# Norms behind the out-projection, a buffer for the meta keys, and three steps of linear attention on ScalarE

## The chip, the core and the metric

The kernel runs on one core of a Trainium2 chip. Its engines are TensorE (PE, with its weight loads as PEld), VectorE (DVE), ScalarE (ACT), GpSimd (POOL) and SyncE (SP, which issues nearly all DMAs). The metric is the device time of one execution in microseconds. Every matmul of a projection works in float32 precision by splitting each operand into a rounded high part and a low rest and adding three products.

## The reference

Sixteen meta tokens are put ahead of 2048 tokens of width 1024, and two layers follow, each with a residual and a layer norm:

```
conv layer:  u = h @ w_in + b_in;  a, ga, z = split(u, 3)
             c = causal depthwise conv, 31 taps, of a * sigmoid(ga)
             y = (silu(layer_norm(c)) * silu(z)) @ w_out + b_out
GLA layer:   q, k, v, r, a1 = split(h @ w_in);   4 heads, 128 wide in q and k, 256 in v
             g = log_sigmoid(a1 @ w_a2 + b_a) / 16;   b = cumsum of g in a chunk of 64
             o = (q exp(b)) @ S + att @ v,  att[t,s] = sum_d q k exp(b_t - b_s), s <= t
             S = exp(b_last) S + (k exp(b_last - b)).T @ v     (chunk by chunk)
             o = o * rsqrt(mean(o*o) + 1e-6) * norm_g;  y = (o * silu(r)) @ w_out
both:        h = layer_norm(alpha * h + y);   the meta tokens are dropped at the end
```

## The kernel before

The program has four phases. In phase 1 (to about 555 us) the input projection and the convolution run, and their results `c` and `silu(z)` go to DRAM (`c_d`, `sz_d`), channels on partitions. Phase 2 (about 555 to 783 us) takes 17 tiles of tokens (`SUBS`: 16 of 128 and one of 16). Phase 3 (to about 1544 us) is the GLA layer without its out-projection, and phase 4 does that and the last norm.

A tile of phase 2 goes through these steps. `norm` loads `c`, sums over the 8 channel groups (DVE for even tiles, POOL's `tree` for odd ones) and over partitions by a matmul with a constant matrix (`mean`), subtracts, squares on ACT, sums again (POOL), gets the variance by a matmul (L330), forms the reciprocal root on POOL, puts it on a diagonal `dg`, and spreads it over partitions by the matmul `rb` (L335); DVE multiplies `c` by it (L336). `gate` does eight Silus on ACT (L351), multiplies with `silu(z)` on DVE (L354) and splits the product into `h_gt` (ACT, L73) and `l_gt` (DVE, L74). `out_proj` multiplies both by the weights (tiles `pj_y`, 48 matmuls of 512 columns for a tile of tokens, L106 to L108), adds the residual (L377) and does the post-LN (L385 to L398), whose result is stored to `h1_d`. The loop L428 to L435 writes these steps down in the order norm of a later tile, gate of a later tile, out-projection of this one; `head` has by then written down three norms (CB is 4) and one gate.

Phase 3 has 4 blocks of tokens (528, then 3 of 512) and 4 heads, so 16 units, named block_head. `proj_units` writes down the projections and, interleaved, a generator `gla_units` is stepped; two numbers (GRATE, VCOST) set how often. A unit computes the decays (`gl` and `b`: L634 to L638), for block 0 the state after the 16 meta tokens (`khm`, through a transpose into `dsm`), then `kh` (decayed keys, filled on POOL at L683, multiplied on DVE at L685, transposed by PE as `pk`, split into `k_h` and `k_l`), the state products `ds`, the attention matrix in levels (`A`, POOL, ACT and DVE at L719 to L723; `att` and `red`), their sum `at` (L770, L771), its split `a_h`, `a_l`, and the outputs `o` in two halves of two chunks. Each chunk's squares are summed on ACT (L783) into a scratch that is the front of `kh`. `osb` is normalised (L784 to L789) and transposed by PE (`oT`, L794).

In what order an engine runs its instructions is set by a scheduler at compile time, which goes by the order in which they are written down, by the tile pools' buffers (a tag with `bufs=1` has one buffer) and by its own model of costs. On the chip each engine keeps that order and waits on semaphores.

Of the kernel before, what the change touches and what calls it, by code (L numbers as in the profile page):

```python
# [11 lines left out]
F32 = mybir.dt.float32  # L12
F32R = mybir.dt.float32r
AF = mybir.ActivationFunctionType
ALU = mybir.AluOpType
# [34 lines left out]
class Trunk:  # L50
# [349 lines left out]
    def phase2(self, x_tok, wo, rows, h1_d, tail):  # L400
        nc = self.nc
        left = ExitStack()
        wop = self.pool(left, name="p2w", bufs=1)
        const = self.pool(left, name="p2c", bufs=1)
        tp = self.pool(left, name="p2t", bufs=3)
        sm = self.pool(left, name="p2n", bufs=4)
        self.pm.append(self.pool(self.st2, name="p2q", bufs=1, space=PSUM, side="right"))

        w = self.load_out_w(wo, wop, lambda k: self.raw(f"wo{k}")[:, :D] if k < 2 else self.wrp.tile([P, D], F32, tag="wr", name=f"wor{k}"), "wo")
        self.st2w.close()  # L410
        rb = []
        for i in range(3):
            t = const.tile([P, D], F32, name=f"row{i}")
            nc.sync.dma_start(t, rows[i : i + 1].broadcast_to([P, D]))
            rb.append(t)
        b_out, g1, b1 = rb

        def out_proj(i, h, l):
            t0, m = SUBS[i]
            xt = tp.tile([P, D], F32, tag="xt", name=f"xt{i}")  # L420
            nc.sync.dma_start(xt[:m], x_tok[t0 : t0 + m])
            self.out_tile(h, l, w, xt, m, f"y{i}")
            nc.gpsimd.tensor_tensor(xt[:m], xt[:m], b_out[:m], op=ALU.add)
            self.post_ln(sm, xt, m, g1, b1, f"a{i}")
            nc.sync.dma_start(h1_d[t0 : t0 + m], xt[:m])

        ns = len(SUBS)
        for i in range(ns):  # L428
            self.norm_next()
            self.gate_next()  # L430
            if self.nnorm == ns and not self.normed and self.st2:
                self.st2.close()
                self.st2 = None
                tail()
            out_proj(*self.gated.popleft())  # L435
        left.close()


# [18 lines left out]
    def phase3_init(self, wa2, pp, og_d):  # L457
        nc = self.nc
        self.og_d = og_d
        c0 = self.pool(self.st3, name="p3a", bufs=1)  # L460
        self.a1x = [c0.tile([P, P], F32, name=f"a1x{i}") for i in range(2)]
        for t in self.a1x:
            nc.gpsimd.memset(t, 0.0)
        self.hp = self.pool(self.st3, name="p3h", bufs=2)
        c = self.pool(self.st3, name="p3c", bufs=1)
        self.prm = c.tile([P, 8], F32, name="prm3")
        nc.sync.dma_start(self.prm[:, 0:6], pp)
        nc.vector.tensor_scalar(self.prm[:, 6:8], self.prm[:, 4:6], 0.5, None, op0=ALU.mult)

        raw = self.raw("a2")[:, :512]  # L470
        nc.sync.dma_start(raw, wa2)
        self.wa2 = c.tile([P, 512], F32R, name="a2")
        nc.scalar.activation(self.wa2, raw, AF.Copy)
        nc.vector.tensor_tensor(self.wa2[64:96], raw[64:96], self.wa2[64:96], op=ALU.subtract)
        with ExitStack() as st:
            self.gla_consts(c, self.pool(st, name="p3k", bufs=1))
        self.gp = self.pool(self.st3, name="p3g", bufs=2)
        self.S = {}
# [147 lines left out]
    def gates(self, bi, h, hd, ns):  # L626
        nc, n = self.nc, BLOCKS[bi][1]
        gl = self.hp.tile([P, BMAX], F32, tag="gl", name=f"gl{bi}_{h}", bufs=1)
        b = hd["b"] = self.hp.tile([P, BMAX], F32, tag="b", name=f"b{bi}_{h}")
        ba = self.prm[:, h : h + 1]  # L630
        for c0, m in ns:
            ps = self.pjt(f"z{bi}_{h}_{c0}")[:, :m]
            nc.tensor.matmul(ps, lhsT=self.wa2[:, h * P : (h + 1) * P], rhs=self.ah[:, c0 : c0 + m], start=True, stop=True)
            nc.vector.tensor_scalar(gl[:, c0 : c0 + m], ps, ba, 0.0, op0=ALU.add, op1=ALU.min)  # L634
            nc.scalar.activation(b[:, c0 : c0 + m], ps, AF.Abs, bias=ba)
        nc.scalar.activation(b[:, :n], b[:, :n], AF.Exp, scale=-1.0)
        nc.scalar.activation(b[:, :n], b[:, :n], AF.Ln, bias=1.0)
        nc.vector.tensor_tensor(gl[:, :n], gl[:, :n], b[:, :n], op=ALU.subtract)  # L638
        o = n - 512
        rs = self.reset.rearrange("p a b -> p (a b)")  # L640
        if o:
            nc.vector.tensor_tensor_scan(b[:, :o], rs[:, :o], gl[:, :o], 0.0, op0=ALU.mult, op1=ALU.add)
        nc.vector.tensor_tensor_scan(b[:, o : o + 512], rs, gl[:, o : o + 512], 0.0, op0=ALU.mult, op1=ALU.add)
# [7 lines left out]
    def gla_units(self, h, hd, bi, t0, n):  # L651
# [3 lines left out]
        off = n - 512  # L655
        if off:

            kh = self.gp.tile([P, 512], F32, tag="kh", name=f"khm{h}", bufs=1)[:, :off]
            nc.gpsimd.tensor_tensor(kh, b[:, off - 1 : off].to_broadcast([P, off]), b[:, :off], op=ALU.subtract)
            ex(kh, kh)  # L660
            nc.vector.tensor_tensor(kh, kh, k_[:, :off], op=ALU.mult)
            pt = self.pt.tile([P, 4, P], F32, tag="g", name=f"ptm{h}")
            nc.tensor.transpose(pt[:off, 0], kh, K.ident)
            kt = self.gp.tile([NMETA, P], F32, tag="ktm", name=f"ktm{h}", bufs=1)
            nc.scalar.activation(kt, pt[:off, 0], AF.Copy)
            ds = self.pa.tile([P, 4, P], F32, tag="ds", name=f"dsm{h}").rearrange("p a b -> p (a b)")[:, :256]
            nc.tensor.matmul(ds, lhsT=kt, rhs=hd["vm"], start=True, stop=True)
            S = self.S[h] = self.gp.tile([P, 256], F32, tag=f"S{h}", name=f"Sm{h}", bufs=1)
            nc.vector.tensor_copy(S, ds)
            yield  # L670
# [79 lines left out]
        for c2 in range(2):  # L750
            sm = self.pt.tile([P, 2, 144], F32, tag="g", name=f"sm{nm}_{c2}")

            for c in range(2):
                a = (2 * c2 + c) * P
                blocks = [(s, slice(a + s, a + s + 32)) for s in range(0, P, 32)]
                for i, m in enumerate((8, 4, 2)):
                    for s, w in blocks:
                        nc.tensor.matmul(sm[s : s + 32, c, 48 + 32 * i : 80 + 32 * i], lhsT=lv[m][:, w], rhs=lv[m][:, w], start=True, stop=True, skip_group_check=True)
                for s, w in blocks:
                    nc.tensor.matmul(sm[s : s + 32, c, :48], lhsT=ks[:, w], rhs=A1[:, (a + s) // 32], start=True, stop=True, skip_group_check=True)  # L760
            ms = self.gp.tile([P, 2, 144], F32, tag="ms", name=f"ms{nm}_{c2}")
            nc.vector.tensor_tensor(ms, sm, K.lmask.unsqueeze(1).to_broadcast([P, 2, 144]), op=ALU.mult)
            rd = red[:, 2 * c2 : 2 * c2 + 2]
            nc.vector.tensor_reduce(rd, ms[:, :, 16:].rearrange("p c (l t) -> p c t l", t=32), axis=mybir.AxisListType.X, op=ALU.add)
            odd = rd.rearrange("p c (s u) -> p c s u", u=2)[:, :, :, 1]
            nc.vector.tensor_tensor(odd, odd, ms[:, :, :16], op=ALU.add)
            yield
        at = self.gp.tile([P, 4, 4, 32], F32, tag="at", name=f"at{nm}", bufs=1)
        for c in range(4):
            nc.vector.tensor_tensor(at[:, c], red[:, c].unsqueeze(1).to_broadcast([P, 4, 32]), K.blk, op=ALU.mult)  # L770
        nc.vector.tensor_tensor(at, at, att.rearrange("p c (a b) -> p c a b", b=32), op=ALU.add)  # L771
        ath, atl = self.pair3("a", at.rearrange("p c a b -> p c (a b)"), nc.gpsimd, nm, 1)
        yield
        yield
# [1 line left out]
        sq = self.gp.tile([P, 3, 4], F32, tag="sq", name=f"sq{nm}")  # L776
        junk = kh[:, :256]
        for c2 in range(2):
            o2 = self.pt.tile([P, 2, 256], F32, tag="g", name=f"o{nm}_{c2}")
            for c in (2 * c2, 2 * c2 + 1):  # L780
                o = o2[:, c % 2]
                self.mm3(o, [(qh[:, c], ql[:, c], *Ss[c]), (ath[:, c], atl[:, c], vh[:, c], vl[:, c])])
                nc.scalar.activation(junk, o, AF.Square, accum_out=sq[:, 0, c : c + 1])  # L783
            nc.vector.tensor_copy(osb[:, 2 * c2 : 2 * c2 + 2], o2)  # L784
            yield
        nc.vector.tensor_scalar(sq[:, 1], sq[:, 0], 1.0 / 256, RMS_EPS, op0=ALU.mult, op1=ALU.add)
        nc.gpsimd.tensor_tensor(sq[:, 2], sq[:, 1], self.mhalf, op=ALU.pow)
        for c in range(4):
            nc.vector.tensor_scalar(osb[:, c], osb[:, c], sq[:, 2, c : c + 1], None, op0=ALU.mult)  # L789
        yield  # L790
        for e in range(2):
            pt = self.pt.tile([P, 4, P], F32, tag="g", name=f"oT{nm}_{e}")
# [165 lines left out]
```

## Time and profile before

| | |
|---|---|
| median of 3 runs | 1737.01 us (1736.24 to 1739.46) |
| the profiled execution | 1736.39 us, span 1734.4 us |
| mean granted TensorE clock | 0.992 of full speed |
| PE busy | 1679.1 us, 97% |
| DVE, POOL, ACT busy | 1396.5 us, 938.4 us, 841.4 us |

The span runs from the first instruction to the last. Busy times of engines overlap, so they don't add up. The clock is a share of 2.4 GHz; its lower level is 1.2 GHz. In the views below, a wait is idle time of an engine that ended when the named instruction of another one was done. A name such as `pj_y` in the trace stands for all buffers of that name, so a tile's number doesn't show there; it is found by counting.

### The profile page before, as it was taken

To read this page: it belongs to the slowest core of one execution; us is meant where nothing else is said; L and a number is where in the kernel's file an instruction comes from. 1 tells how busy PE (TensorE), PEld (TensorE's weight loads), DVE (VectorE), ACT (ScalarE), POOL (GpSimd) and SP (SyncE) were. 2 spreads that over 40 slices of the span, in tenths; PEclk is the share of its full clock that TensorE was granted. 3 is DMA by queue.
4 is the path that set the end of the run, shared out by engine and by line. 5 is a ranking of instruction groups with operands and counts; after the bars stand their busy time and mean duration, and the time that the engine had idled before them with its cause. 6 is when DMAs were issued, how large, how long until landed. Compare 5 with 4: busy or idle time off the path is not lost.

```text
span 1734.4 us, 29031 instructions
## 1 busy us (share of the span) xinstructions
PE 1679.1 (97%) x11715; PEld 1491.7 (86%) x11715; DVE 1396.5 (81%) x1869; ACT 841.4 (49%) x1269; POOL 938.4 (54%) x675
## 2 busy tenths in 40 slices
PE   8999999999998998999999999999999999999998
PEld 8999999999998776778888888888888888788886
DVE  5789999999998898877776787777887788787665
ACT  6445555655544544445545454555555465541000
POOL 1879999999985788766332243332443153331000
PEclk9999999999999999999999999999999999999999
DMA  7110111111146644443122322223223322355441
GB/s 247 37 37 37 37 69 42 74 52 59 72 146 206 207 148 142 142 139 106 50 86 87 111 84 88 74 87 111 78 75 106 123 74 84 126 170 169 147 134 61
DMA packets 103910, 178.72 MB, mean 103 GB/s; under 512 B 8624, under 2 KB 68400, under 8 KB 103776
## 3 DMA queue, kind: packets, MB, share of 16 engines
q1 hardware_dynamic: 103776, 176.86, 30.4%
q8 instruction: 92, 1.51, 0.4%
q14 instruction: 42, 0.34, 0.1%
HBM read 134.70 MB, written 42.14 MB: 102 GB/s over the span
## 4 chain that ended last, share of the span: by engine, by line
PE 69%; DVE 12%; POOL 8%; ACT 5%; issue 3%; DMA 3%; SPq 0%; DVEq 0%; POOLq 0%; ACTq 0%
PE pj_y L106 4%; PE pj_y L108 4%; PE pj_y L107 4%; PE pj_g L107 3%; PE pj_g L108 3%; PE pj_g L106 3%; PE pj_z L107 3%; PE pj_z L106 3%; PE pj_a L107 3%; PE pj_a L106 3%; PE pj_z L108 3%; PE pj_a L108 3%; POOL A L720 1%; POOL A L719 1%; PE att L729 1%
## 5 line engine op out<-in xcount | busy, mean ns | idle before, releaser
L196 POOL TENSOR_TENSOR gacc<-gacc,prod 128x1024 f32<-128x1024 f32 (+1 forms) x156 | 385.9, 2477 | 63.1 <-ACT prod L195 54.2
L204 DVE SCALAR_TENSOR_TENSOR cacc<-glu,prm,cacc 128x1024 f32<-128x1024 f32 (+1 forms) x292 | 374.8, 1294 | 7.0
L195 ACT ACTIVATE prod<-glu,prm 128x1024 f32<-128x1024 f32 (+1 forms) x156 | 179.1, 1155 | 107.7 <-POOL gacc L196 107.3
L719 POOL TENSOR_TENSOR A<-b 128x256 f32<-128x256 f32 x96 | 80.2, 836 | 269.9 <-PE att L729 105.6
L106 PE MATMUL pj_g<-xh,h_w 128*128 128x412 f32 (+1 forms) x320 | 113.7, 355 | 5.6 <-ACT h_w L73 4.2
L107 PE MATMUL pj_g<-xl,h_w 128*128 128x412 f32 (+1 forms) x320 | 113.5, 355 | 0.3 <-DVE xl L74 0.3
L108 PE MATMUL pj_y<-woh,l_gt 128*128 128x512 f32 (+1 forms) x272 | 109.0, 406 | 4.3 <-DVE l_gt L74 4.2
L106 PE MATMUL pj_y<-woh,h_gt 128*128 128x512 f32 (+1 forms) x272 | 110.7, 410 | 1.9 <-ACT h_gt L73 1.8
L108 PE MATMUL pj_g<-xh,l_w 128*128 128x412 f32 (+1 forms) x320 | 112.5, 353 | 0.0
L107 PE MATMUL pj_z<-xl,h_w 128*128 128x412 f32 (+1 forms) x320 | 112.3, 351 | 0.0
L106 PE MATMUL pj_z<-xh,h_w 128*128 128x412 f32 (+1 forms) x320 | 112.2, 351 | 0.0
L107 PE MATMUL pj_a<-xl,h_w 128*128 128x412 f32 (+1 forms) x320 | 112.2, 351 | 0.0
L106 PE MATMUL pj_a<-xh,h_w 128*128 128x412 f32 (+1 forms) x320 | 112.1, 350 | 0.0
L108 PE MATMUL pj_z<-xh,l_w 128*128 128x412 f32 (+1 forms) x320 | 112.0, 351 | 0.0
L108 PE MATMUL pj_a<-xh,l_w 128*128 128x412 f32 (+1 forms) x320 | 111.9, 350 | 0.0
L107 PE MATMUL pj_y<-wol,h_gt 128*128 128x512 f32 (+1 forms) x272 | 110.6, 406 | 0.0
L106 PE MATMUL pj_y<-w4h,h_g 128*128 128x512 f32 x256 | 99.9, 391 | 0.0
L107 PE MATMUL pj_y<-w4l,h_g 128*128 128x512 f32 x256 | 99.8, 390 | 0.0
L108 PE MATMUL pj_y<-w4h,l_g 128*128 128x512 f32 x256 | 99.7, 389 | 0.0
L388 POOL TENSOR_TENSOR rs<-rs,mhalf 128x1 f32<-128x1 f32 x16 | 14.8, 923 | 155.7 <-DVE rs L387 155.7
L377 DVE SCALAR_TENSOR_TENSOR xt<-xt,pj_y 128x512 f32<-128x512 f32 (+1 forms) x66 | 44.5, 677 | 59.2 <-PE pj_y L108 59.2
L654 ACT ACTIVATE A<-A 128x512 f32<-128x512 f32 (+1 forms) x112 | 66.3, 597 | 46.0 <-POOL A L720 43.1
(428 smaller groups left out, 5264.0 us busy)
## 6 DMA issues: line engine op xcount, KB each, us to landing
r_w<-w SPq DMA_DIRECT2D x24, 512.0 KB, 3.2
c<-c_d SPq DMA_DIRECT2D x16, 512.0 KB, 4.5
szb<-sz_d SPq DMA_DIRECT2D x16, 512.0 KB, 4.6
xt<-x_tok SPq DMA_DIRECT2D x16, 512.0 KB, 4.5
h_d<-xt SPq DMA_DIRECT2D x16, 512.0 KB, 2.7
r_h1b<-h_d SPq DMA_DIRECT2D x16, 512.0 KB, 3.6
og_d<-og SPq DMA_DIRECT2D x32, 256.0 KB, 3.9
xt<-h_d SPq DMA_DIRECT2D x16, 512.0 KB, 3.5
```

Source lines behind the costliest of these rows:

```text
L106: mm(out, lhsT=lh, rhs=rh, start=(i == 0), stop=False)
L107: mm(out, lhsT=lh, rhs=rl, start=False, stop=False)
L108: mm(out, lhsT=ll, rhs=rh, start=False, stop=(i == n - 1))
L195: nc.scalar.activation(pr, src(k), AF.Copy, scale=tap(k))
L196: nc.gpsimd.tensor_tensor(st["g"], st["g"], pr, op=ALU.add)
L204: nc.vector.scalar_tensor_tensor(out, src(k), tap(k), acc, op0=ALU.mult, op1=ALU.add)
L377: self.nc.vector.scalar_tensor_tensor(xt[:m, es], xt[:m, es], ALPHA, ps, op0=ALU.mult, op1=ALU.add)
L388: nc.gpsimd.tensor_tensor(rs[:n, 2:3], rs[:n, 1:2], self.mhalf[:n, 0:1], op=ALU.pow)
L654: ex = lambda o, i: nc.scalar.activation(o, i, AF.Exp, scale=1.0 / TAU)
L719: nc.gpsimd.tensor_tensor(Av[:, :, 0], mid, bv[:, :, 0], op=ALU.subtract)
L720: nc.gpsimd.tensor_tensor(Av[:, :, 1], bv[:, :, 1], mid, op=ALU.subtract)
L729: nc.tensor.matmul(att[s : s + m, c, s + m : s + 2 * m], lhsT=A[:, a : a + m], rhs=A[:, a + m : a + 2 * m], start=False, stop=False, skip_ ...
```

## The change

It has three parts. In phase 2 the loop writes a later tile's norm down behind the out-projection. The meta tokens' decayed keys get a tile of their own tag, `khm`, 16 columns wide. In the GLA units, `gl` is formed as Relu(-z - b_a) by ACT, with the sign turned in the subtraction; `at` starts as ACT's copy of `att` and `red` is added to its diagonal blocks by four additions on 32 partitions each; and `osb` is written by ACT straight from PSUM with the reciprocal root as scale, half by half, so that the power on POOL is taken twice a unit, for two chunks each.

```diff
@@ phase2, loop over the tiles
-            self.norm_next()
             self.gate_next()
...
             out_proj(*self.gated.popleft())
+
+            self.norm_next()
@@ phase3_open
+        self.nba = c.tile([P, 4], F32, name="nba3")
+        nc.vector.tensor_scalar(self.nba, self.prm[:, 0:4], -1.0, None, op0=ALU.mult)
@@ the decays
-            nc.vector.tensor_scalar(gl[:, c0 : c0 + m], ps, ba, 0.0, op0=ALU.add, op1=ALU.min)
+            nc.scalar.activation(gl[:, c0 : c0 + m], ps, AF.Relu, bias=self.nba[:, h : h + 1], scale=-1.0)
...
-        nc.vector.tensor_tensor(gl[:, :n], gl[:, :n], b[:, :n], op=ALU.subtract)
+        nc.vector.scalar_tensor_tensor(gl[:, :n], gl[:, :n], -1.0, b[:, :n], op0=ALU.mult, op1=ALU.subtract)
@@ gla_units
-            kh = self.gp.tile([P, 512], F32, tag="kh", name=f"khm{h}", bufs=1)[:, :off]
+            kh = self.gp.tile([P, off], F32, tag="khm", name=f"khm{h}", bufs=1)
...
-        for c in range(4):
-            nc.vector.tensor_tensor(at[:, c], red[:, c].unsqueeze(1).to_broadcast([P, 4, 32]), K.blk, op=ALU.mult)
-        nc.vector.tensor_tensor(at, at, att.rearrange("p c (a b) -> p c a b", b=32), op=ALU.add)
+        nc.scalar.activation(at.rearrange("p c a b -> p (c a b)"), att.rearrange("p c t -> p (c t)"), AF.Copy)
+        for a in range(4):
+            rows = slice(32 * a, 32 * (a + 1))
+            nc.vector.tensor_tensor(at[rows, :, a], at[rows, :, a], red[rows], op=ALU.add)
...
-            nc.vector.tensor_copy(osb[:, 2 * c2 : 2 * c2 + 2], o2)
+            nc.vector.tensor_scalar(sq[:, 1, cs], sq[:, 0, cs], 1.0 / 256, RMS_EPS, op0=ALU.mult, op1=ALU.add)
+            nc.gpsimd.tensor_tensor(sq[:, 2, cs], sq[:, 1, cs], self.mhalf[:, cs], op=ALU.pow)
+            for c in (2 * c2, 2 * c2 + 1):
+                nc.scalar.activation(osb[:, c], o2[:, c % 2], AF.Copy, scale=sq[:, 2, c : c + 1])
             yield
-        nc.vector.tensor_scalar(sq[:, 1], sq[:, 0], 1.0 / 256, RMS_EPS, op0=ALU.mult, op1=ALU.add)
-        nc.gpsimd.tensor_tensor(sq[:, 2], sq[:, 1], self.mhalf, op=ALU.pow)
-        for c in range(4):
-            nc.vector.tensor_scalar(osb[:, c], osb[:, c], sq[:, 2, c : c + 1], None, op0=ALU.mult)
```

The order of the instructions moves on every engine. Three places follow; a name such as `rb6_5051` is the tile `rb` of token tile 6 with a buffer number behind, and the line numbers are those of the version shown.

PE's order just ahead of the out-projection of tile 6, before:

```order
L106 MATMUL pj_y5_1_5227<-woh7_4637,h_gt5_5093 128x512
L107 MATMUL pj_y5_1_5227<-wol7_4638,h_gt5_5093 128x512
L108 MATMUL pj_y5_1_5227<-woh7_4637,l_gt5_5094 128x512
L335 MATMUL rb7_5073<-dg7_5078,mean_80 128x128
L330 MATMUL rb8_5175<-mean_80,sq8_5166 128x1
L106 MATMUL pj_y6_0_5305<-woh0_4595,h_gt6_5195 128x512
L107 MATMUL pj_y6_0_5305<-wol0_4596,h_gt6_5195 128x512
```

And after the change:

```order
L107 MATMUL pj_y5_1_5207<-wol7_4638,h_gt5_5071 128x512
L108 MATMUL pj_y5_1_5207<-woh7_4637,l_gt5_5072 128x512
L335 MATMUL rb6_5051<-dg6_5056,mean_80 128x128
L323 MATMUL mean8_5250<-sq8_5248,mean_80 128x128
L330 MATMUL rb7_5155<-mean_80,sq7_5144 128x1
L106 MATMUL pj_y6_0_5283<-woh0_4595,h_gt6_5175 128x512
L107 MATMUL pj_y6_0_5283<-wol0_4596,h_gt6_5175 128x512
```

Before, `rb6` stands 35 instructions ahead of `pj_y6_0`, and `rb7` and `rb8` directly ahead; now it is `rb6` itself, with two small matmuls between.

PE's order just ahead of the out-projection of tile 15 (`trb0` are transposes of the first block's input to phase 3), before:

```order
L106 MATMUL pj_y14_1_6133<-woh7_4637,h_gt14_6019 128x512
L107 MATMUL pj_y14_1_6133<-wol7_4638,h_gt14_6019 128x512
L108 MATMUL pj_y14_1_6133<-woh7_4637,l_gt14_6020 128x512
L106 MATMUL pj_y15_0_6299<-woh0_4595,h_gt15_6101 128x512
L107 MATMUL pj_y15_0_6299<-wol0_4596,h_gt15_6101 128x512
L106 MATMUL pj_y15_1_6325<-woh0_4595,h_gt15_6101 128x512
```

And after:

```order
L108 MATMUL pj_y14_1_6133<-woh7_4637,l_gt14_6000 128x512
L335 MATMUL rb15_5979<-dg15_5984,mean_80 128x128
L335 MATMUL rb16_6081<-dg16_6086,mean_80 128x16
L498 MATMUL trb0_0_0_6213<-ident_73,r_h1b0_0_6211 128x128 x4
L498 MATMUL trb0_0_1_6220<-ident_73,r_h1b0_0_6211 128x128 x4
L498 MATMUL trb0_128_0_6229<-ident_73,r_h1b0_128_6227 128x128 x4
L106 MATMUL pj_y15_0_6299<-woh0_4595,h_gt15_6101 128x512
L107 MATMUL pj_y15_0_6299<-wol0_4596,h_gt15_6101 128x512
```

Before, `rb15` stands 50 instructions ahead of `pj_y15_0`; now it stands behind the last product of tile 14, with `rb16` and three groups of transposes between it and tile 15.

POOL's order in the first GLA unit (`khm0` is the meta tokens' tile, `kh0_0` the unit's keys, `A0_0_16` a level of its attention), before, where `khm0` stands five rows above the first one shown:

```order
L719 TENSOR_TENSOR A0_0_16_6956<-b0_0_6730 128x16x16
L720 TENSOR_TENSOR A0_0_16_6956<-b0_0_6730 128x16x16
L719 TENSOR_TENSOR A0_0_8_7013<-b0_0_6730 128x32x8
L720 TENSOR_TENSOR A0_0_8_7013<-b0_0_6730 128x32x8
L743 TENSOR_TENSOR A10_0_7031<-b0_0_6730 128x16x16
L746 COPY A10_0_7031<-b0q0_6750 128x16x32
L74 TENSOR_TENSOR q_l0_0_6833<-eb0_0_6823,q_h0_0_6832 128x512
L683 TENSOR_TENSOR kh0_0_6827<-b0_0_6730 128x512
```

And after:

```order
L662 TENSOR_TENSOR khm0_6813<-b0_0_6732 128x16
L686 TENSOR_TENSOR kh0_0_6829<-b0_0_6732 128x512
L722 TENSOR_TENSOR A0_0_64_6883<-b0_0_6732 128x4x64
L723 TENSOR_TENSOR A0_0_64_6883<-b0_0_6732 128x4x64
L722 TENSOR_TENSOR A0_0_32_6902<-b0_0_6732 128x8x32
```

`kh0_0` has moved from behind eight `A` instructions, the two of `A10_0` and `q_l0_0` to the place directly behind `khm0`.

## Rows read from the trace of the kernel before

**Rows 1.** Page, part 1: busy us (share of the span) and instructions, by engine.

```profile
PE 1679.1 (97%) x11715; PEld 1491.7 (86%) x11715; DVE 1396.5 (81%) x1869; ACT 841.4 (49%) x1269; POOL 938.4 (54%) x675
```

**Rows 2.** Windows, phase 2: us, busy PE, PEld, DVE, ACT, POOL, clock, DMA, GB/s.

```profile
615.00:702.50 87.50, 77.18 (x328) 60.17 (x327) 76.84 (x96) 42.14 (x72) 75.49 (x56) 0.96 0.46 145
702.50:802.50 100.00, 99.93 (x526) 78.58 (x525) 78.46 (x119) 44.48 (x81) 66.75 (x60) 1.00 0.41 133
```

**Rows 3.** Waits of PE, 600 to 800 us: total, times, longest.

```profile
PE pj_y L108 <- DVE l_gt L74: 3.9, 3, 2.5
```

**Rows 4.** Windows of the GLA phase, columns as in rows 2.

```profile
827.50:840.00 12.50, 9.88 (x97) 9.15 (x98) 8.03 (x14) 3.40 (x7) 1.65 (x3) 0.73 0.25 85
860.00:1510.00 650.00, 631.62 (x6091) 543.20 (x6090) 500.64 (x873) 343.19 (x616) 222.75 (x245) 1.00 0.27 91
1510.00:1544.00 34.00, 31.52 (x233) 28.30 (x234) 24.08 (x38) 18.18 (x32) 14.95 (x17) 0.95 0.51 176
```

**Rows 5.** Timeline of PE in the first GLA unit: start, us, [idle before].

```profile
830.12 1.12 PE L693 MATMUL pk<-ident,kh 128*128 128x128 f32 x4 [3.86 <-DVE kh L685]
...
836.56 0.38 PE L108 MATMUL ds<-vhb0v,k_l 128*128 128x256 f32 x1
```

**Rows 6.** Waits of PE, 860 to 1544 us.

```profile
PE ds L106 <- DVE Sm L707: 4.7, 2, 3.2
PE o L106 <- ACT a_h L73: 3.7, 2, 2.5
PE o L106 <- ACT kh L783: 3.6, 4, 1.7
PE o L108 <- POOL a_l L74: 2.8, 4, 0.8
```

**Rows 7.** Timeline of PE, two neighbouring products of an out-projection.

```profile
565.27 0.39 PE L106 MATMUL pj_y<-woh,h_gt 128*128 128x512 f32 x1
565.50 0.39 PE L107 MATMUL pj_y<-wol,h_gt 128*128 128x512 f32 x1
```

**Rows 8.** Timeline of tile 6: DVE first, then ACT.

```profile
627.54 1.22 DVE L336 TENSOR_TENSOR c<-c,rb 128x1024 f32<-128x1024 f32 x1 [0.35 <-PE rb L335]
...
633.90 1.06 ACT L73 ACTIVATE h_gt<-c 128x1024 fp32r<-128x1024 f32 x1 [1.92 <-DVE c L354]
```

**Rows 9.** Timeline of tile 15: PE, DVE, ACT.

```profile
745.09 0.49 PE L335 MATMUL rb<-dg,mean 128*128 128x128 f32 x2
...
748.91 2.50 DVE L397 TENSOR_TENSOR xt<-xt,row 128x1024 f32<-128x1024 f32 x1
...
755.07 1.06 ACT L73 ACTIVATE h_gt<-c 128x1024 fp32r<-128x1024 f32 x1 [2.86 <-DVE c L354]
```

**Rows 10.** Timeline of the first GLA unit: POOL, then DVE.

```profile
814.15 0.95 POOL L659 TENSOR_TENSOR khm<-b 128x16 f32<-128x16 f32 x1 [5.37 <-DVE b L642]
...
824.61 1.22 POOL L683 TENSOR_TENSOR kh<-b 128x512 f32<-128x512 f32 x1
...
832.60 0.68 DVE L74 TENSOR_TENSOR k_l<-pk,k_h 128x512 fp32r<-128x512 f32 x1
```

**Rows 11.** Lines, 860 to 1600 us: busy us, mean ns, idle before.

```profile
L783 ACT ACTIVATE kh<-o 128x256 f32<-128x256 f32 x63 | 24.1, 382 | 64.3 <-PE o L108 63.7
L784 DVE COPY osb<-o 128x512 f32<-128x512 f32 x32 | 21.8, 685 | 18.7 <-ACT kh L783 18.7
...
L789 DVE TENSOR_SCALAR osb<-osb,sq 128x256 f32<-128x256 f32 x64 | 21.0, 391 | 1.2 <-POOL sq L787 1.2
...
L787 POOL TENSOR_TENSOR sq<-sq,mhalf 128x4 f32<-128x4 f32 x16 | 18.4, 1152 | 5.0 <-DVE sq L786 3.1 <-DVE khm L661 1.2
...
L770 DVE TENSOR_TENSOR at<-red,blk 128x128 f32<-128x128 f32 x60 | 16.5, 311 | 0.3
```

**Rows 12.** Timeline of unit 1_3: DVE, then POOL.

```profile
1208.25 0.28 DVE L786 TENSOR_SCALAR sq<-sq 128x4 f32<-128x4 f32 x1
...
1215.17 1.19 POOL L787 TENSOR_TENSOR sq<-sq,mhalf 128x4 f32<-128x4 f32 x1
```

More of the change, by code (lines that the diff above doesn't have):

```diff
@@ L778, in gla_units @@
         for c2 in range(2):
+            cs = slice(2 * c2, 2 * c2 + 2)
             o2 = self.pt.tile([P, 2, 256], F32, tag="g", name=f"o{nm}_{c2}")
```

## The prediction

> **What bounds the kernel now.** First the page's table of busy times [rows 1]: PE is busy for 97% of the span, so whatever the other engines do, the change can win at most PE's gaps and what a lowered clock costs. It removes no matmul. PE issues strictly in the order fixed at compile time, so I then read, stage by stage, how long PE stands idle, what clock it was granted and what it waited for.
>
> In the conv layer's second half (norm, gate, out-projection) PE is busy 77.18 of 87.5 us in the first part, at a mean granted clock of 0.96, and 99.93 of 100 us in the rest [rows 2]. So 10.3 us of gaps and about 87.5 × 0.04 = 3.4 us of clock can be won there, 13.7 us together. The waits behind the gaps are small ones; the largest sum is 3.9 us for the split's l_gt [rows 3].
>
> In the GLA phase the first unit has a hole of its own: a 3.86 us wait for kh, and a mean clock of 0.73 over 12.5 us [rows 4, 5]. Behind it PE is busy 631.62 of 650 us, then 31.52 of 34 at clock 0.95 [rows 4]: 18.4 + 2.5 + 34 × 0.05 = 22.6 us that can be won. The largest waits there are for Sm (DVE), for a_h and a_l (the attention's split), and for the squares L783 [rows 6]. DVE is busy 500.64 of those 650 us (77%), ACT 343.19 (53%), POOL 222.75 (34%).
>
> All sums are against the profiled execution, 1736.39 us (span 1734.4 and 2.0 around it); it lies 0.6 us below the median of the runs, 1737.01, so no correction is made.
>
> **Part 1, norms behind the out-projection (term A).** This part adds no instruction and moves many. On SP the loads of c, sz and x nearly keep their places (the ninth c load now precedes the first store of h instead of following it); I cost the DMAs at nothing, since the loads run about three tiles ahead, and if that lead were short, PE would wait for part of a load. What matters is PE's order. Before, rb6 stands 35 PE instructions ahead of y6's first matmul; one of 512 columns takes 0.23 us (565.27 to 565.50 [rows 7]), so some 8 us of PE work lie between. Now two small matmuls lie between, about 0.6 us. The same happens to rb15 and y15: 50 instructions or 11.5 us before, and now rb16 and three groups of transposes, about 1.7 us.
>
> From rb to y runs a chain on other engines: DVE multiplies (L336), ACT does eight Silus, DVE multiplies with the gate, ACT rounds to h_gt. Tile 6 takes from 627.54 to 633.90 + 1.06 = 634.96, 7.4 us, and at most 0.35 more from rb [rows 8]; I take 7.6. Tile 15 takes from rb's end, 745.58, to 756.13: 10.5 us, of which 2.5 is a DVE instruction of another tile (L397) and 2.86 ACT's wait for DVE [rows 9]. So y6 must wait 7.6 − 0.6 = 7.0 us (9.9 with the slow chain), and y15 between 7.6 − 1.7 = 5.9 and 8.8, say 7. Behind the waiting y stands every later matmul; the engines it waits for are not held. A gap is followed by a stretch at the lower of the clock's two levels (1.2 of 2.4 GHz): around the 3.86 us gap, 12.5 us had a mean of 0.73 [rows 4, 5], a loss of up to 12.5 × 0.27 = 3.4. I take 2.2 after each, since the gap itself is part of that stretch. Together 14 + 4.4 = 18.4. The other tiles get longer leads (at least 9.8 us of PE work between rb and y, where the shortest of before was 7.9), so their waits should go; I leave 2 us for what stays. A = 18.4 + 2 − 13.7 = **+7**. Bounds: with chains of 7.4, nothing left of other waits and no clock lost, 6.8 + 5.7 − 13.7 = −1, and −3 if DVE, free while y waits, speeds the chain by a tenth or so; with chains of 10.5, clock 2 × 3.4 and 8 us of old waits, 9.9 + 8.8 + 6.8 + 8 − 13.7 = +20. I stay near tile 6's row, since PE's wait takes work from DVE's queue.
>
> **Part 2, the meta keys' own buffer (term B).** Before, the POOL instruction that fills kh waits until the meta tokens' 16 columns have left the shared buffer: it runs at 824.61, ten us behind khm's at 814.15, and PE gets kh at 830.12 [rows 5, 10]. Now POOL's order has kh directly behind khm, so that wait of 3.86 us goes. Then another operand is late: the third product of ds needs k_l, made by DVE at 832.60 to 833.28 [rows 10] and used by PE at 836.56 [rows 5]. DVE's work ahead of k_l is the same, so it can come only some 0.4 us earlier and the product at about 832.5: 4 us. The A pieces on POOL, moved behind kh, come 1.22 us later. B = **−4**; +1.2 at one end (the A pieces become the wait, nothing else gained), 3.86 and the 2.2 of clock, −6, at the other. The other units have no khm; there kh waits as before for the squares that use its buffer.
>
> **Part 3, gl, at and osb from DVE to ACT (term C).** From the rows of these lines [rows 11], a unit loses on DVE: two copies and four scalings, 2 × 0.685 + 4 × 0.391 = 2.93; four block multiplies, 4 × 0.311 = 1.24; and the addition to at and the first step of gl, each 512 columns wide like the copies, 2 × 0.68 = 1.36. It gains four additions on 32 partitions (at 0.311 at most 1.24) and a second L786 (0.28 [rows 12]). Net 5.5 − 1.5 = 4.0 us of some 42 a unit. ACT gains four copies of 256 columns at L783's 0.382 and two of 512 (Relu, att) at no more than twice that: 3.0 us. POOL gains one power of 1.152. What covers these is ACT's 47% and POOL's 66% of free time; uncovered, each would cost PE its length once a unit. The subtraction L638 only changes its form: nothing.
>
> What ends earlier: behind the last red the attention path had 1.24 + 0.68 us on DVE and now has 1.24, since the copy of att can go ahead. Sm waits in DVE's queue behind less work. What ends later: the outputs. The transposes of the first half now stand 3.8 to 7.4 us of PE work behind that half's last product (counted as above). The path is square 0.382, L786 0.28, power 1.152, two copies 0.76, so 2.6 us with some 0.2 for each of five hand-offs, 3.6; if the next unit's kh (1.22) stands between on POOL, 4.8. POOL can hold a power longer: in unit 1_3 L786 ended at 1208.53 and the power began at 1215.17, behind A pieces [rows 12]. Most units are covered, a few by tenths only.
>
> Of PE's waits, Sm 4.7, a_h 3.7 and a_l 2.8, 11.2 us together [rows 6], lie on paths that get shorter. I take half, 5.6, and 1.4 of the 1.7 us of clock: C = **−7**. Bounds: all of them and the squares' 3.6, −15; half a us lost at the transposes of each of 16 units, +8.
>
> **Sum.** 1736.4 + 7 − 4 − 7 = 1732.4, so 1732. Its own range, with half of each term's spread, is 1724 to 1739.
>
> **Rivals.**
> *Everything pays.* If y6 and y15 find the quick end (A = +3), the first unit gains 5 and the GLA phase 14, the time is 1736.4 − 16 = 1720. For it speaks that 22.6 us of gaps stand there and that DVE loses nearly a tenth of its work; against it, that a relieved wait of PE often meets the next late operand, as k_l above.
>
> *Slower: the two late rb.* If DVE puts other tiles' work between, as L397 did in tile 15 [rows 9], both chains take 10.5 us: A = 9.9 + 8.8 + 6.8 + 6 − 13.7 = +18. With B and C as forecast that is 1743. It decides from A = +15 on. For it: DVE is busy 76.84 of 87.5 us just there [rows 2]. Against it: while y waits, no new out-projection reaches DVE.
>
> *DVE's relief is worth nothing.* DVE has 23% of its time free in the GLA phase, and PE's waits may hang on the length of chains, not on DVE's load: Sm's 4.7 us are two waits in sixteen units [rows 6]. Then C = 0 and the time is 1739.4. The Trainium skill says in "Perfetto Trace Analysis", section "Optimizing Scalar/DVE Operations", that moving work to Scalar may make sense if DVE is saturated, and that where neither is, but bubbles arise elsewhere, instructions should be broken up. By that rule this rival would be the forecast. The trace agrees with its condition, since DVE is at 77%; no run so far shows what a relief of DVE is worth here.
>
> **How the numbers follow.** A measurement of this kernel tells 0.2%, 3.5 us, from no change, so 1733.5 to 1740.5 counts as the same. Forecast 0.45 (by its own range 0.25 faster, 0.17 same, 0.03 slower); everything pays 0.19, all faster; late rb 0.18, all slower; no worth in the relief 0.18 (0.15 same, 0.03 slower by its spread). Faster 0.44, same 0.32, slower 0.24. The range takes in the rivals' times and a few us past them, for the ends of A and C: 1717 to 1747.
>
> **What would show it.** A: gaps of about 7 us on PE ahead of y6 and y15, each with a low clock behind it, and no other wait over 1 us in that stage. B: the wait for kh gone, and the third product of ds at about 832.5, shifted by A. C: idle time of PE in the GLA phase lower by a third, DVE some 64 us less busy in all, ACT 48 more, transposes oT waiting under 0.5 us. Wrong it would be with no such gaps ahead of y6 and y15, with the A pieces as the first unit's new wait, or with a wait for osb at most units.

## The result, and the profile after

The changed kernel takes 1755.88 us (median of 4 runs, 1753.67 to 1757.13) against 1736.62 us (4 runs, 1734.48 to 1739.46): 1.0097 times, interval 1.0081 to 1.0113. That is 19 us slower, outside the forecast range of 1717 to 1747 and on the side of the second rival. The profiled execution took 1755.89 us, its span 1754.2. Part 1 of the page:

```profile
PE 1678.8 (96%) x11715; PEld 1492.7 (85%) x11715; DVE 1352.9 (77%) x1754; ACT 880.7 (50%) x1369; POOL 943.5 (54%) x691
```

Against [rows 1] PE's work is the same. DVE lost 43.6 us and ACT gained 39.3, smaller than the 64 and 48 forecast. The forecast added up durations, and those of DVE do sum to 59.6 us less. But neighbours overlap: in the DVE rows of tile 6 below, the row at 637.16 ends at 638.38 and the next begins at 638.30. Busy time counts such a stretch once. All of the loss is PE standing still or running slowly, so the first thing to find is where. The table says how much later a tile's last product ends in the trace after than in that of before, tile by tile:

| PE's products of | lag, us | what lies between |
|---|---|---|
| y0, y5 | 0.8, 1.4 | start of phase 2 |
| y6, y7 | 12.0, 12.2 | a jump of 10.6 |
| y11, y14 | 3.6, 5.3 | old waits that went, and some new ones |
| y15, y16 | 16.7, 16.7 | a jump of 11.4 |
| first projection behind the first unit (q of head 1) | 11.9 | a gain of 4.8 |
| last projection to q (block 3, head 3) | 18.7 | the other units |
| last of phase 4 | 19.8 | |

So term A was 16.7 − 0.8 = +15.9, B was 11.9 − 16.7 = −4.8, and C was 19.8 − 11.9 = +7.9, where +7, −4 and −7 had been forecast.

The windows of phase 2 (columns as in rows 2):

```profile
615.00:702.50 87.50, 72.43 (x316) 57.62 (x315) 73.25 (x89) 40.18 (x68) 68.54 (x55) 0.94 0.47 146
702.50:802.50 100.00, 90.69 (x412) 68.08 (x412) 74.69 (x105) 42.66 (x79) 61.49 (x48) 0.95 0.38 122
```

The second window was full before [rows 2]; now it has 9.3 us of gaps and a clock of 0.95. What PE waited for from 550 to 815 us:

```profile
PE pj_y L106 <- ACT h_gt L73: 11.4, 3, 9.6
PE trb L498 <- DMA r_h1b<-h_d: 4.1, 1, 4.1
PE mean L323 <- DVE sq L321: 3.8, 1, 3.8
PE trb L498 <- DVE c L336: 2.8, 1, 2.8
PE rb L330 <- POOL sq L343: 2.4, 1, 2.4
PE rb L335 <- DVE dg L334: 1.8, 1, 1.8
```

One wait of 9.6 us stands out. The timelines around it, ahead of y6, PE first, then DVE, then ACT, then POOL:

```profile
636.21 0.38 PE L335 MATMUL rb<-dg,mean 128*128 128x128 f32 x2
...
646.57 0.79 PE L106 MATMUL pj_y<-woh,h_gt 128*128 128x512 f32 x1 [9.64 <-ACT h_gt L73]
647.16 0.63 PE L107 MATMUL pj_y<-wol,h_gt 128*128 128x512 f32 x1
...
637.16 1.22 DVE L397 TENSOR_TENSOR xt<-xt,row 128x1024 f32<-128x1024 f32 x1 [1.31 <-ACT xt L396]
638.30 0.68 DVE L377 SCALAR_TENSOR_TENSOR xt<-xt,pj_y 128x512 f32<-128x512 f32 x1
638.90 1.21 DVE L336 TENSOR_TENSOR c<-c,rb 128x1024 f32<-128x1024 f32 x1
...
643.37 2.06 DVE L354 TENSOR_TENSOR c<-c,szb 128x1024 f32<-128x1024 f32 x1 [2.06 <-ACT c L351]
...
640.15 3.19 ACT L351 ACTIVATE c<-c,prm 128x128 f32<-128x128 f32 x8 [3.02 <-DVE c L336]
...
645.46 1.06 ACT L73 ACTIVATE h_gt<-c 128x1024 fp32r<-128x1024 f32 x1 [1.18 <-DVE c L354]
...
642.00 2.34 POOL L423 TENSOR_TENSOR xt<-xt,row 128x1024 f32<-128x1024 f32 x1
```

The chain is the forecast one, but it is the slow one: `rb6` is there at 636.6, and DVE first has to wait for ACT and do two instructions of tiles 4 and 5, so that L336 begins at 638.90; later L354 takes 2.06 us, with POOL's L423 beside it, where that of tile 15 below takes 1.21. PE has nothing to issue ahead of y6. The products behind the gap take 0.63 us each where those of [rows 7] take 0.39: after standing still PE was granted 0.50 of the clock, its lower level, and the same happens behind the gap at y15 (columns as in rows 2):

```profile
646.50:649.50 3.00, 2.93 (x9) 2.43 (x10) 2.97 (x5) 0.02 (x1) 3.00 (x4) 0.50 0.62 175
773.00:777.00 4.00, 4.00 (x9) 2.76 (x10) 4.00 (x5) 3.72 (x6) 1.39 (x1) 0.50 0.00 0
```

The timelines ahead of y15, PE, then DVE, then ACT, then the DMA queue of SP:

```profile
766.38 1.30 PE L498 MATMUL trb<-ident,r_h1b 128*128 128x128 f32 x8 [2.81 <-DVE c L336]
771.81 1.12 PE L498 MATMUL trb<-ident,r_h1b 128*128 128x128 f32 x4 [4.13 <-DMA r_h1b<-h_d]
773.00 0.80 PE L106 MATMUL pj_y<-woh,h_gt 128*128 128x512 f32 x1
...
763.37 1.23 DVE L397 TENSOR_TENSOR xt<-xt,row 128x1024 f32<-128x1024 f32 x1 [1.31 <-ACT xt L396]
764.51 0.68 DVE L377 SCALAR_TENSOR_TENSOR xt<-xt,pj_y 128x512 f32<-128x512 f32 x1
765.11 1.41 DVE L336 TENSOR_TENSOR c<-c,rb 128x1024 f32<-128x1024 f32 x2
...
770.58 1.21 DVE L354 TENSOR_TENSOR c<-c,szb 128x1024 f32<-128x1024 f32 x1
...
771.88 1.26 ACT L73 ACTIVATE h_gt<-c 128x1024 fp32r<-128x1024 f32 x2
...
767.71 0.32 SPq L493 DMA_DIRECT2D r_h1b<-h_d  x1
```

From the end of `rb` at 763.6 to y15 at 773.0 are 9.4 us. The same two DVE instructions, here of tiles 13 and 14, stand ahead of L336. The transposes that were to fill the gap wait themselves, first behind L336 and then for a DMA, until h_gt is nearly there. That DMA was issued at 767.71, when the eight transposes ahead of it had ended (766.38 + 1.30). So two paths run from L336 to y15, over the gate to h_gt and over the transposes and the load, and both end at about 772.9.

In the first unit POOL's keys now follow `khm` at once, and PE's wait for kh is gone. POOL, then PE:

```profile
830.23 0.95 POOL L662 TENSOR_TENSOR khm<-b 128x16 f32<-128x16 f32 x1 [6.70 <-DVE b L645]
831.32 1.04 POOL L686 TENSOR_TENSOR kh<-b 128x512 f32<-128x512 f32 x1
...
840.64 0.49 PE L696 MATMUL pk<-ident,kh 128*128 128x128 f32 x3
...
848.42 0.39 PE L108 MATMUL ds<-vhb0v,k_l 128*128 128x256 f32 x1 [1.13 <-DVE k_l L74]
```

The next late operand is k_l, as forecast; 848.42 is 11.9 us behind the 836.56 of [rows 5], where the lag had been 16.7.

PE's waits in the other units (876 to 1560 us), which answer to [rows 6]:

```profile
PE o L106 <- DVE xlb L501: 4.6, 2, 2.6
PE o L106 <- ACT a_h L73: 4.4, 3, 2.6
PE o L108 <- POOL a_l L74: 3.3, 4, 2.5
PE ds L106 <- DVE Sm L710: 3.2, 2, 2.1
PE oT L799 <- ACT osb L793: 3.2, 4, 1.3
PE o L106 <- ACT kh L789: 3.1, 5, 0.7
```

Sm, a_h and a_l had 11.2 us before and have 10.9. Two lines grew, the transposes' wait for osb and the wait of the outputs o behind the split of the next block's input on DVE. In the kernel before (860 to 1544 us) they were

```profile
PE oT L794 <- DVE osb L789: 0.9, 2, 0.4
...
PE o L106 <- DVE xlb L498: 0.4, 1, 0.4
```

The edited lines (876 to 1616 us):

```profile
L793 ACT ACTIVATE osb<-o,sq 128x256 f32<-128x256 f32 x62 | 25.9, 471 | 19.3 <-POOL sq L791 19.2
...
L791 POOL TENSOR_TENSOR sq<-sq,mhalf 128x2 f32<-128x2 f32 x31 | 22.2, 716 | 64.9 <-DVE sq L790 64.6
L776 DVE TENSOR_TENSOR at<-at,red 32x128 f32<-32x128 f32 x60 | 22.2, 370 | 0.8
...
L773 ACT ACTIVATE at<-att 128x512 f32<-128x512 f32 x15 | 8.9, 594 | 5.3 <-PE att L732 5.3
```

An addition on 32 partitions takes 370 ns, more than a block multiply on 128 [rows 11]; so the at step relieves DVE of 1.92 − 4 × 0.37 = 0.4 us a unit and not of 0.7. And ACT stands still for 19 us in its order at the scaled copies until POOL's power is there.

### The profile page after: what moved, and what is told of

Read it like the earlier page. It is cut to its first block, busy times and chain, and to the rows that moved or that the text cites. A ratio compares the mean times of both kernels' runs of the same rounds, so it can differ in the third digit from the quotient of the medians.

```text
span 1754.2 us, 29040 instructions
## 1 busy us (share of the span) xinstructions
PE 1678.8 (96%) x11715; PEld 1492.7 (85%) x11715; DVE 1352.9 (77%) x1754; ACT 880.7 (50%) x1369; POOL 943.5 (54%) x691
## 4 chain that ended last, share of the span: by engine, by line
PE 70%; DVE 13%; ACT 6%; POOL 5%; issue 3%; DMA 3%; SPq 0%; DVEq 0%; POOLq 0%; ACTq 0%
PE pj_y L107 4%; PE pj_y L106 4%; PE pj_y L108 4%; PE pj_g L107 3%; PE pj_g L108 3%; PE pj_g L106 3%; PE pj_z L107 3%; PE pj_z L106 3%; PE pj_a L107 3%; PE pj_a L106 3%; PE pj_z L108 3%; PE pj_a L108 3%; DVE A L726 2%; DVE A L725 1%; DMA c<-c_d 1%
## 5 line engine op out<-in xcount | busy, mean ns | idle before, releaser
L722 POOL TENSOR_TENSOR A<-b 128x256 f32<-128x256 f32 x96 | 84.2, 877 | 238.7 <-PE att L732 141.6
L106 PE MATMUL pj_y<-woh,h_gt 128*128 128x512 f32 (+1 forms) x272 | 110.8, 410 | 11.5 <-ACT h_gt L73 11.4
```

Of the source, the lines that this page charges most:

```text
L106: mm(out, lhsT=lh, rhs=rh, start=(i == 0), stop=False)
L722: nc.gpsimd.tensor_tensor(Av[:, :, 0], mid, bv[:, :, 0], op=ALU.subtract)
```

## The experiments

Medians of before went from 1737.98 to 1738.71 us in these runs, so each result is told by its ratio, with 1738 us as the base of the differences.

**Each part alone.** `norm_only` is before with the loop of the change:

```diff
-            self.norm_next()
             self.gate_next()
...
             out_proj(*self.gated.popleft())
+
+            self.norm_next()
```

> The kernel before with only the norm written down behind the out-projection. Theory 1 (the cost of phase 2 is the two late rb): y6 and y15 wait 9 to 10 us each and the clock falls behind them, as in the changed kernel; 16 us slower than before, 1752 to 1754, and the GLA phase as long as before. Theory 2 (the order of phase 2 only costs together with the GLA phase's new order): less than half of it, under 1745. Theory 3 (phase 3's added gaps come from phase 2's new order too): the whole +19, 1755 or more.

Measured: 1753.11 us, 1.0080 (1.0068 to 1.0092), 14 us slower. In its trace y6 waits less than theory 1 says, 8.1 us, and the transposes ahead of y15 wait as in the changed kernel (600 to 810 us):

```profile
PE pj_y L106 <- ACT h_gt L73: 8.8, 2, 8.1
PE trb L496 <- DMA r_h1b<-h_d: 3.6, 1, 3.6
PE trb L496 <- DVE c L336: 2.8, 1, 2.8
```

`gla_only` has all the rest of the change and not this.

> The kernel before with all of the change but the norms. Theory 1 (the parts add up): first unit 4 to 5 us faster, the rest of the GLA phase 8 us slower: 1738 to 1742. Theory 3 (the GLA phase is slower because of phase 2's order): the first unit's gain alone, 1731 to 1733.

Measured: 1743.81 us, 1.0024 (1.0014 to 1.0034), 4 us slower. The two add up to 18 of the 19 us: phase 2 and phase 3 each have a loss of their own, and theories 2 and 3 fall. The trace of `gla_only`, counted as in the table above, gains 4.2 us across the first unit and loses 7.8 behind it, so terms B and C come out without the norms as in the changed kernel (−4.8 and +7.9). Behind the first products of the first unit `norm_only` has the order of before on PE and DVE, and it loses 0.7 us between y16 and the end.

`khm_only` changes one line (as in the change, tag `khm`, 16 columns).

> The kernel before with only the meta keys' own buffer. Theory 1: the wait of 3.86 us for kh and its low clock go, nothing else moves: 1731 to 1733. Rival (the A pieces behind kh on POOL become the next wait, or the order of later units moves): 1735 or more.

Measured: 1737.39 us, 0.9985 (0.9977 to 0.9994), 2.6 us faster, the one part that pays; it is the fastest version found that computes all. Of the wait of 3.86 us, 1.6 comes back elsewhere: PE's longest wait of its first unit (815 to 860 us) is

```profile
PE dsm L667 <- ACT ktm L665: 1.6, 1, 1.6
```

where `ktm` is the copy of the transposed meta keys, which the wait for kh had covered.

**One late rb taken back.** `norm_but_12`, against before:

```diff
         for i in range(ns):
-            self.norm_next()
+            if i in (12,):
+                self.norm_next()
             self.gate_next()
...
             out_proj(*self.gated.popleft())
+            if i not in (12,):
+                self.norm_next()
```

> As the run with the norms alone, but in the loop's round 12 the norm is written down ahead of gate and out-projection, as before; rb15 then stands 11.2 us of PE work ahead of y15, by matmuls counted in PE's order, and rb6 still directly ahead of y6. Theory 1 (each late rb is paid for by itself): the step of 10 us at y15 goes and that at y6 stays: 1743 to 1746, 4 to 7 us above before. Theory 2 (the norms' new place costs as a whole, through DVE and POOL): 1749 or more.

Measured: 1747.77 us, 1.0055 (1.0042 to 1.0068), 9.6 us above before, 4.3 less than `norm_only`. PE's waits in it, 600 to 810 us:

```profile
PE pj_y L106 <- ACT h_gt L73: 10.7, 2, 9.7
PE rb L330 <- POOL sq L343: 3.9, 2, 2.0
PE rb L335 <- DVE dg L334: 2.0, 1, 2.0
```

The wait of y6 stays at 9.7 us and that of y15 is gone, as theory 1 says; but the variance of tile 15 and h_gt of tile 13 are now late, and the lag grows by 4.7 us there, from y12 to y13. So the time lies between the two theories: a late rb has its own price, and in this order the moved norm cost some us elsewhere.

**at.** `at_only` has that edit alone.

> The kernel before with only at formed from ACT's copy of att and four additions on 32 partitions. Theory 1 (the path to a_h is shorter, DVE has less to do): 0 to 3 us faster than before. Rival (ACT takes the copy late, so a_h is later): 2 to 4 us slower, with longer waits of PE for a_h.

Measured: 1746.51 us, 1.0048 (1.0033 to 1.0063), 8 us slower: the theory is wrong, and the rival named the wrong wait. PE's waits, 860 to 1550 us:

```profile
PE o L106 <- ACT kh L784: 7.0, 10, 1.4
...
PE o L106 <- DVE xlb L498: 4.0, 3, 2.7
PE o L106 <- ACT a_h L73: 3.9, 4, 1.9
```

a_h is waited for as before, though its path got shorter: from the last red to the end of a_h, mean of 16 units, 4.2 us before and 2.9 here. PE's order shows where that went. Between the last product of the attention levels and the first product with a_h stood 9.4 us of PE work before, and 8.1 here (counted at 0.23 us for 512 columns, mean of 16 units; 7.8 in the changed kernel). So the new order has moved the consumer forward by what the operand gained. What grew are the waits of a chunk's first products, of q with the state: behind ACT's squares (L784) 7.0 us against 3.6 [rows 6], and behind the split xlb 4.0 against 0.4. The trace loses 6.1 us from y16 to the end. Squares and split both read PSUM, where o is written; that PE waits there for the memory and not for an operand is likely, but no run shows it. `at_on_dve` takes the copy of att on DVE, here against `at_only`:

```diff
-        nc.scalar.activation(at.rearrange("p c a b -> p (c a b)"), att.rearrange("p c t -> p (c t)"), AF.Copy)
+        nc.vector.tensor_copy(at.rearrange("p c a b -> p (c a b)"), att.rearrange("p c t -> p (c t)"))
```

> The at step with the copy of att taken by DVE and not by ACT; the four additions on 32 partitions stay. DVE's load is about that of before (0.68 + 4 x 0.36 against 4 x 0.31 + 0.67), ACT's is unchanged. Theory A (the cost comes from PE's new order, 431 of 4586 instructions out of the common one): 4 to 9 us slower than before, like at_only. Theory B (the cost is ACT's added 0.59 us a unit): within 2 us of before.

Measured: 1752.02 us, 1.0078 (1.0062 to 1.0094), 14 us slower, more than either theory allows. So theory B falls: without ACT's copy the step costs no less. PE's order differs here too, so the run doesn't show what the copy costs by itself.

**osb.** `osb_only` has that edit alone; `half_on_dve` scales on DVE instead of ACT; `act_copy` only moves the unscaled copies:

```diff
# half_on_dve, against osb_only
-                nc.scalar.activation(osb[:, c], o2[:, c % 2], AF.Copy, scale=sq[:, 2, c : c + 1])
+                nc.vector.tensor_scalar(osb[:, c], o2[:, c % 2], sq[:, 2, c : c + 1], None, op0=ALU.mult)
# act_copy, against before
-            nc.vector.tensor_copy(osb[:, 2 * c2 : 2 * c2 + 2], o2)
+            nc.scalar.activation(osb[:, 2 * c2 : 2 * c2 + 2], o2, AF.Copy)
```

> The kernel before with only osb normalised by ACT from PSUM, half by half. Theory 1 (this part makes the GLA phase's new gaps, by waits of the transposes for osb and of the next products for PSUM or ACT): 5 to 9 us slower, 1741 to 1746, with waits of oT for osb of 3 us in all. Rival (the new gaps come from the att or gl step): within 2 us of before.

> The kernel before with osb normalised from PSUM half by half, as in the change, but by DVE. Theory 1 (the cost of that part is ACT, which stands still in its order until POOL's power is there, and holds up what is queued behind): the wait moves to DVE, which has one instruction less a unit; within 2 us of before. Theory 2 (the cost is the power taken twice and the transposes moved forward, whoever scales): 3 to 6 us slower than before, like the run with ACT.

> The kernel before with only the copies of o from PSUM moved from DVE to ACT, unscaled; power and scaling stay as they were, on POOL and DVE. Theory 1 (ACT's wait for the power is the cost): without that wait ACT has room, within 2 us of before or up to 3 faster. Theory 3 (ACT's added time is the cost, the wait is idle time it could spare): 3 us slower or more.

Measured: `osb_only` 1743.92 us, 1.0026 (1.0016 to 1.0035), 4.5 us slower; `half_on_dve` 1740.44 us, 1.0012 (1.0004 to 1.0021), 2 us slower; `act_copy` 1746.26 us, 1.0043 (1.0028 to 1.0058), 7.5 us slower. `half_on_dve` is near theory 1, though its interval overlaps that of `osb_only`. But ACT's wait for the power can't be the whole cause: without it, in `act_copy`, more is lost, and there the transposes wait for osb (860 to 1550 us), 5.6 us against 0.9 before:

```profile
PE oT L794 <- DVE osb L789: 5.6, 6, 2.2
```

By that run theory 3 (ACT's time) holds; `plain_act_copy` below speaks against it.

**gl, and the version that would be best.** `gl_only` has the Relu, `khm_gl` both it and the buffer.

> The kernel before with only gl formed by ACT's Relu. If the parts' times add up (all GLA edits +4.2, khm -2.6, osb +4.5, at +8.3, from the ratios), this one must be 6 us faster than before, 1732. If they don't add up because each edit reorders PE anew and loses some us by that (theory A), it is 3 to 8 us slower, like the others.

> The meta keys' own buffer and gl by Relu together, the version that would beat both kernels if the parts add up: 8 us faster than before, 1730. By theory A: 0 to 6 us slower.

Measured: 1742.93 us, 1.0022 (1.0012 to 1.0032), and 1741.43 us, 1.0016 (1.0006 to 1.0027). Alone the four GLA edits cost −2.6 + 3.8 + 8.3 + 4.5 = +14 us, together +4: the parts don't add up (for the buffer and gl alone the sum, +1.2, and the measured +2.8 lie within their intervals), and no combination of them run here beats `khm_only`.

**Relief without load.** `no_scale` leaves the outputs unnormalised:

```diff
-        for c in range(4):
-            nc.vector.tensor_scalar(osb[:, c], osb[:, c], sq[:, 2, c : c + 1], None, op0=ALU.mult)
```

> The kernel before without the four scalings of osb a unit, so the outputs are left unnormalised: DVE has 1.56 us a unit less to do, 25 us in all, nobody has more, and the transposes wait for less. Theory A (PE's new order, 415 instructions out of the common one, decides): no faster than before, 0 to 8 us slower. Theory B (relief of DVE pays and load on ACT costs): 3 to 8 us faster.

Measured: 1735.59 us, 0.9979 (0.9968 to 0.9991), 3.6 us faster, as theory B says, at its lower end. The four scalings take 25 us by their durations, and DVE's busy time falls by 17.9, from 1396.5 to 1378.6 us. So relief that is given away for nothing, and that shortens the path to the transposes as well, is worth a fifth of that.

**The order.** `order_only` is before with GRATE 2.6, `gla_order` is `gla_only` with it.

> The kernel before with GRATE 2.6 in place of 2.7: the same instructions on every engine, but the GLA units are interleaved with the projections a little differently, and 566 of PE's 4586 instructions leave the common order, about as many as with one edit. Theory A (PE's new order, not the work, costs): 3 to 10 us slower than before. Theory B: within 2 us of before.

> All GLA edits with GRATE 2.6: the same work as the run gla_only, 463 of PE's 4586 instructions out of the order common with it. Theory A (the order decides, by several us in either direction): 3 us or more away from gla_only's 1.0024. Theory B (the work decides): within 2 us of it, 1.0012 to 1.0036.

Measured: 1740.14 us, 1.0014 (1.0005 to 1.0023), and 1744.86 us, 1.0039 (1.0025 to 1.0053). The same work in another order costs 2.4 us, between what the two theories said. `gla_order` lies 2.6 us above `gla_only`, but their intervals overlap. So an order changed by about as much as by one edit can cost 2 us, and what the single edits cost beyond that is not explained by it.

Then the scheduler's other mode, on before and three edits:

```diff
-    with _tile.TileContext(nc, schedule_with_timeline_sim=True) as tc:
+    with _tile.TileContext(nc, schedule_with_timeline_sim=False) as tc:
```

> The kernel before with the scheduler's other mode, in which its model of engine times is off and the order follows the text more closely. It is the base for the next three. No theory on its own time; I expect 1750 to 1900 us, since many products then stand ahead of their operands.

> The at step alone in that mode. PE's order in the GLA phase is then nearly that of its base (36 of 4586 instructions out of the common order, against 412 in the run at_only). Theory A (the GLA phase got slower because the edits made the scheduler put PE's work in another order, whose waits are worse): within 2 us of its base or faster by up to 5. Theory B (the work itself, now on ACT, is late): 6 to 10 us slower than its base.

> The unscaled copies of o on ACT in that mode; 42 instructions out of the common order, against 378 in the run act_copy. Theory A: within 2 us of its base or faster by up to 5. Theory B: 5 to 9 us slower than its base.

> All of the GLA edits in that mode; 119 instructions out of the common order, against 652 in the run gla_only. Theory A: faster than its base by 5 us or more, since the first unit's gain of 3 to 5 stays and DVE has 44 us less to do. Theory B: 2 us slower than its base or more.

Measured: 2051.45 us for the base (1.1798 of before, 1.1766 to 1.1831, far above what I expected), then 2059.44 (1.1832 to 1.1867), 2050.95 (1.1781 to 1.1818) and 2048.67 (1.1770 to 1.1811). So the at step costs 8 us here too, just clear of the base, and the −0.5 of the copies on ACT and the −2.8 of the GLA edits are not clear of no change. The traces say more. They are 3 to 5 us behind the base's at y0 already, where no edit acts, so I count from y16 to PE's last product:

| edit | usual mode, us | this mode, us |
|---|---|---|
| at | +6.1 | +3.9 |
| copies of o on ACT | +4.3 | −4.3 |
| all GLA edits | +3.6 | −11.5 |

With PE's order nearly kept, the copies and the edits together cost nothing, which speaks for the order as their price. It is one trace each, and the base has many other waits, so these differences need not carry over one to one. For the at step, which loses in both modes, the order explains a part at most.

## Why the prediction was wrong

The changed kernel came 23.5 us above the forecast: 9 of them are term A's, 15 term C's, and B was 1 better than forecast. The forecast's own range, 1724 to 1739, does not follow from its bounds: halved and added up they give 1722 to 1749.

**Term A, mechanism right, sizes wrong.** y6 and y15 stand behind a late rb and PE waits for the forecast chain. Two terms of the sum were mis-sized. One is the chain: I took 7 us for each gap, near tile 6's quick row, "since PE's wait takes work from DVE's queue". The post-LN of the tile two before and the residual of the last one were already in that queue, ahead of L336 in DVE's order, so both gaps came at the slow chain: 9.6 and 9.4 us. With the clock the two jumps of the lag are 10.6 and 11.4, 22.0 in place of 18.4. At y15, "I cost the DMAs at nothing" looked at the loads of phase 2 and not at that of r_h1b, which by the trace held y15 till about the same time as h_gt; no run parts the two. The other term, and the larger miss, is "I leave 2 us for what stays". Of the 13.7 us of old losses only 12.2 − 5.3 = 6.9 came back between y7 and y14, so by this count 6.8 stayed or came anew: rb waited 1.8 us for dg, a mean 1.1 and two tiles 1.8 for h_gt. 22.0 − 6.9 and some tenths make +15.9. That is the rival of the two late rb, which put A at +18; its time, 1743, took C as forecast.

**Term B, right.** The wait for kh went, k_l was next, −4.8 in the changed kernel. Alone the part gives −2.6, since the copy ktm then comes late.

**Term C, wrong in sign.** The failing step is "I take half" of the waits for Sm, a_h and a_l, which "lie on paths that get shorter". The path to a_h did get shorter (red to a_h from 4.2 to 3.3 us in the changed kernel), but the three waits stayed at 10.9 of 11.2 us. In the new order the consumers stand earlier too: 9.4 us of PE work ahead of the first a_h product became 7.8. The transposes of the first half, which stood 8.3 us of PE work behind the unit's last o product, now follow it by 1.2 on average. That the scheduler did this because the operands come earlier is argued. A wait that is left was here no reserve that a shorter path uses up, and new waits came on top: osb from 0.9 to 3.2 us, xlb from 0.4 to 4.6. That +7.9 agrees with the upper bound of +8 is luck: the bound had all of it at the transposes.

The rival that DVE's relief is worth nothing was nearly right: `no_scale` finds 3.6 us for 17.9 of DVE's busy time. The Trainium skill ("Perfetto Trace Analysis", section "Optimizing Scalar/DVE Operations") says that offloading to Scalar may make sense where DVE is saturated. The runs agree so far as that a DVE that was busy for 77% gave those 3.6 us when relieved.

**What stays open.** That the copies of o cost by PE's order is made likely by one pair of runs, and not shown. Why the at step costs 8 us in either mode, and 14 with the copy on DVE, is open: its own path is shorter, its DVE time a little less, and the waits that grow are those behind ACT's squares and xlb. Nor can the +7.9 of the GLA phase be divided among its edits, since they don't add up.

## What to carry to other kernels

Where a change at compile time puts a producer directly ahead of its consumer on an in-order engine, price the gap by the whole chain with what already stands in the other engines' queues, and take its slow instance. And don't stop at the gap that you forecast: the same move can put other operands late, as it did here for rb, a mean and h_gt. Credit a shorter path or a relieved engine with nothing until the order that is built shows that the consumer kept its distance: count the work between the two in the new order, and time each part alone as well as all together, since these parts did not add.

## What was unexpected of the hardware

A DVE addition on 32 partitions of 128 elements took 370 ns, and a multiply on 128 partitions of 128 elements 311 ns: fewer partitions saved nothing, as far as the two operations can be compared. POOL's power took 716 ns for 2 columns and 1152 for 4. The DVE multiply L354 took 1.21 us in tile 15, with POOL idle since 769.35, and 2.06 us in tile 6, where for its first microsecond POOL ran a 1024-column addition, and then a power. One pair of rows does not show that POOL is the cause.
